# Moving a modulation's matrix-vector product from a dilated attention into the units of two feed-forwards

## The chip, the cores and the metric

The kernel runs on one core of a Trainium2 chip. The metric is the time of one execution on the device, in microseconds; the median of three runs of the kernel before is 3267.85 us (3267.14 to 3267.87).

## The reference

Two blocks work on x, 512 tokens of width 1024. The first has two layers, each of a feed-forward, a mixer and a second feed-forward, with a layer norm after each; the mixer is a pooling in layer 0 and a dilated attention in layer 1.

```python
for i in range(DEPTH):                          # DEPTH = 2
    h = _swiglu(x, ffn1_w_gate[i], ffn1_w_up[i], ffn1_w_down[i])
    x = _layer_norm(ALPHA * x + 0.5 * h, ...)
    m = _pool_mixer(...) if i % 2 == 0 else _dilated_attention_mixer(...)
    x = _layer_norm(ALPHA * x + m, ...)
    h = _swiglu(x, ffn2_w_gate[i], ffn2_w_up[i], ffn2_w_down[i])
    x = _layer_norm(ALPHA * x + 0.5 * h, ...)
```

The second block has two layers as well. Each begins with a modulation that depends on the vector c alone, not on x:

```python
mod = silu(c) @ ada_w[l] + ada_b[l]             # 1024 x 3072, l = 0, 1
shift, scale, gate = jnp.split(mod, 3, axis=-1)
h = rms_norm(x, pre_norm[l]) * (1.0 + scale) + shift
...
x = x + gate * rms_norm(y, post_norm[l])
```

So the modulation of both layers can be computed anywhere ahead of the second block. It is small: 24 MB of weights are read and multiplied once.

## The kernel before

**Stages.** The stages run one after the other; in the trace the first feed-forward lies at about 30 to 365 us, the pooling mixer up to 475, the second feed-forward of layer 0 up to 820, the first of layer 1 up to 1172, the dilated attention up to 1800, the last feed-forward up to 2160, then the second block. Tensors are fp32; every product is made as three matmuls of split operands (high and low parts), so TensorE has three matmuls for one product, and each weight must be split: ScalarE writes the high part (wh, L143), VectorE the low one (wl, L145), or GpSimd in one of five parts outside the units. `Stream` loads weights through the SP queue and keeps splits prepared four parts ahead of their use (`split_ahead`, five buffers).

**A feed-forward** (`ffn`, L476 to L601) has eleven units of 256 hidden columns, in four parts (`FF_PARTS`): units 0 to 2, 3 to 5, 6 to 8, 9 and 10. Unit 0 is a plain one (`first_unit`), in which VectorE also makes the sums of token blocks (`token_sums`). Units 1 to 10 use block sums: seven products (`product`, L512) of 24 matmuls of 256 columns each, for which VectorE makes four block sums (`block`, L108), seven splits and seven evacuations. After the units of a part, `f2` multiplies by w_down: two halves of 512 columns, TensorE's tiles t inside the rows kt. The last part's second half ends in the layer norm.

**The dilated attention** (`dilated_mixer`, L768) projects q, k and v for eight pairs of heads (`make_qk`, `make_v`) and attends beside it. For each pair `attend` goes through eight units of 128 queries: products (L880 to L886), scores on VectorE (L901, L904), the exponential on ScalarE (L905), a transposition on TensorE (L912), the weighing (L924, L928), the division (L933, L936) and a second transposition (L943).

**Background work.** `K.bg` takes a generator and a rate; `tick`, called after each three matmuls (as half a tick where they have 256 columns), advances it by the rate and runs the next step for each whole number. What a step issues stands there in the program. A planner then orders the instructions of each engine by when they can run by its own times; so an instruction without an early operand may float forward. `drain` runs what is left; generators with `slow` only when it is asked for these.

**The modulation** (`ada`, L1118 to L1170) is such a generator, started by `begin()` in the attention after the first projection, at 0.43 steps a tick, drained behind the attention. It goes through 24 blocks of 256 columns (12 for each layer). For a block it clears the sum m (L1141), reads the bias into its first row (L1142), and multiplies four quarters of two row tiles: a load of 256 KB through GpSimd's queue (L1132, two buffers adaw, each issued two quarters ahead) and two products on VectorE, whose first line is

```python
nc.vector.scalar_tensor_tensor(m, w[:, n, :], k.cols["c_2"][:, kt:kt + 1], m, ...)   # L1148
```

Then m is split (L1153, L1154), summed over the partitions by two matmuls with ones (L1161, L1162), a row is made on VectorE (L1165 to L1169) and stored (L1170). A block has seven yields; a layer has two more for the first loads. `pin` (L187) makes a tile depend on the latest output of a unit's `factor` in a feed-forward (`k.recent`) by a copy of one element on GpSimd; outside feed-forwards it does nothing.

Of the kernel before, what the change touches and what calls it, by code (L numbers as in the profile page):

```python
# [15 lines left out]
D = 1024  # L16
# [148 lines left out]
class K:  # L165
# [4 lines left out]
    def __init__(self, tc, ctx):  # L170
        self.tc = tc
        self.nc = tc.nc
        sp = lambda n, b, **k: ctx.enter_context(tc.tile_pool(name=n, bufs=b, **k))
        self.const = sp("const", 1)
        self.wraw = sp("wraw", self.raw_bufs)
        self.wraw2 = self.wsum = None
        self.wh = sp("wh", self.split_bufs)
        self.wl = sp("wl", self.split_bufs)
        self.ps = sp("ps", 8, space=PSUM)
        self.pend = []  # L180
        self.bgs = []
        self.recent = None

    def bank(self):
        return self.ps.tile([P, 512], F32, name="bank", tag="bank")
# [16 lines left out]

    def tick(self, w=1.0):
        for e in list(self.bgs):
            e[2] += e[1] * w
            while e[2] >= 1.0:
                e[2] -= 1.0
                try:
                    next(e[0])
                except StopIteration:  # L210
                    self.bgs.remove(e)
                    break
# [263 lines left out]
def ffn(k, st, a, name, i, lnj, post, tail=4):  # L476
    from contextlib import ExitStack
    nc, tc = k.nc, k.tc
    V = nc.vector
    with ExitStack() as ctx:  # L480
        sp = lambda n, b, c=ctx: c.enter_context(tc.tile_pool(name=n, bufs=b, reuse_waits="tile"))
        fa, ft = sp("ffa", 6), sp("fft", 2)
        units = ExitStack()
        k.wraw2, k.wsum, fs = sp("wraw2", k.raw_bufs, units), sp("wsum", 1, units), sp("ffs", 1, units)
        tmp = lambda n, dt: fa.tile([P, 2 * S], dt, name=n, tag="act")
        tp2 = lambda n, b=2: ft.tile([P, S], F32, name=n, tag=n, bufs=b)
        acts, A, later = {}, {}, []

        def new_acts(u):
            acts[u] = [tmp(n, F32R).rearrange("p (a b) -> p a b", a=2) for n in ("ah", "al")]  # L490

        def factor(u, v, o):

            h, lo = [o(x) for x in acts[u]]
            nc.scalar.activation(h, v, AF.Copy)
            V.tensor_tensor(lo, v, f32(h), ALU.subtract)
            k.recent = lo

        def first_unit():
            nonlocal A  # L500
            ps = f1_first(k, st, 4)
            A, later[:] = token_sums(k, fs, tmp)
            new_acts(0)
            for j in range(2):
                g = tp2("ta")
                nc.scalar.activation(g, ps[j], AF.Silu)
                ps[j] = g
            for j in range(2):
                V.scalar_tensor_tensor(ps[j], ps[j], 0.5, ps[2 + j], op0=ALU.mult, op1=ALU.mult)
                factor(0, ps[j], lambda x: x[:, j, :])  # L510

        def product(bank, name, first=False, last=False):  # L512

            h, lo = st.next()
            ah, al = A[name]
            for j in range(2):
                cs = slice(j * P, (j + 1) * P)
                o = bank[:, j * HS:(j + 1) * HS]
                for kt in range(4):
                    for n, (x, y) in enumerate(((h, ah), (h, al), (lo, ah))):  # L520
                        nc.tensor.matmul(o, x[:, kt, cs], y[:, kt, :], start=first and j == kt == n == 0,  # L521
                                         stop=last and kt == 3 and n == 2, skip_group_check=True)
                    k.tick(0.5)

        def unit(u, before):

            R, C = {}, {}
            b = k.bank()
            product(b, "a11", first=True)
            p1 = tp2("ta")  # L530
            nc.scalar.activation(p1, b, AF.Copy)
            before(0)
            ba = k.bank()
            product(ba, "a12", first=True, last=True)
            V.tensor_tensor(p1, p1, ba, ALU.add)
            nc.scalar.activation(p1, p1, AF.Silu)
            before(1)
            if later:
                later.pop(0)()
            product(b, "s2")  # L540
            u2 = tp2("tb")
            nc.scalar.activation(u2, b, AF.Copy)
            bc = k.bank()
            product(bc, "s1", first=True)
            product(b, "s3")
            u3 = tp2("tc")
            nc.scalar.activation(u3, b, AF.Copy)  # L547
            c22 = u3
            V.tensor_tensor(c22, u3, bc, ALU.add)
            if later:  # L550
                later.pop(0)()
            return b, bc, p1, u2, c22

        def rest(u, s, step):
            b, bc, g1, u2, c22 = s
            if u not in acts:
                new_acts(u)
            half = lambda n: lambda x: x[:, :, n * HS:(n + 1) * HS]
            two = lambda x: x.rearrange("p (a b) -> p a b", a=2)
            if step == 0:  # L560
                product(b, "a22", last=True)
                g2 = tp2("td", 1)
                nc.scalar.activation(g2, b, AF.Silu)
                V.scalar_tensor_tensor(c22, g2, 0.5, c22, op0=ALU.mult, op1=ALU.mult)
                factor(u, two(c22), half(1))
            else:
                product(bc, "s4", last=True)
                V.tensor_tensor(u2, u2, bc, ALU.add)
                V.scalar_tensor_tensor(u2, g1, 0.5, u2, op0=ALU.mult, op1=ALU.mult)
                factor(u, two(u2), half(0))  # L570

        for part, (u0, u1) in enumerate(FF_PARTS):
            fin = part == len(FF_PARTS) - 1
            if u0 == 0:
                first_unit()
            held = None
            for u in range(max(u0, 1), u1):
                s = unit(u, (lambda step: None) if held is None else (lambda step: rest(*held, step)))
                held = (u, s)
            rest(*held, 1)  # L580
            rest(*held, 0)
            if fin:
                units.close()
                k.wraw2 = k.wsum = None
                pl, tp = sp("ff", 1), sp("ffl", 2)
            for c in range(2):
                cs = slice(c * 512, (c + 1) * 512)
                if fin and c == 1:
                    G, B = load_gb(k, pl, a, i, lnj)

                def evac(t, ps):
                    x = k.x[t]
                    if part == 0:
                        V.scalar_tensor_tensor(x[:, cs], x[:, cs], ALPHA, ps, op0=ALU.mult, op1=ALU.add)
                    else:
                        V.tensor_tensor(x[:, cs], x[:, cs], ps, ALU.add)
                    if fin and c == 1:
                        k.pend.append(layer_norm_tile(k, tp, t, G, B, post))
                act = lambda kt: [x[:, kt % 2, :] for x in acts[kt // 2]]
                f2(k, st, act, list(range(2 * u0, 2 * u1)), 512, evac, tail=tail if fin and c == 1 else 0)  # L600
        k.recent = None  # L601

# [160 lines left out]
    return res  # L765


def dilated_mixer(k, st, a, lnj, begin):  # L768
    nc, tc = k.nc, k.tc
    slopes = alibi_slopes()  # L770
    with tc.tile_pool(name="dmo", bufs=1, reuse_waits="tile") as po:
        oT = [po.tile([P, S], F32, name=f"oT{i}") for i in range(KT)]
        with tc.tile_pool(name="dm", bufs=1, reuse_waits="tile") as pl, \
# [183 lines left out]
            for kind, n in DIL_ORDER:  # L957
# [3 lines left out]
                    make_qk(n)  # L961
                made.add((kind, n))
                k.drain()
                if len(made) == 1:
                    begin()
                hp = 2 * n if kind == "v" else n
                if ("v", hp // 2) in made and ("qk", hp) in made:
                    last = len(made) == len(DIL_ORDER)
# [149 lines left out]
def ada(k, a, l, out, alloc):  # L1118
# [16 lines left out]
    yield  # L1135
    load(1)
    yield
    for j in range(3 * D // W):
        i, c = j * W // D, j * W % D
        m = alloc("adam", F32)  # L1140
        nc.gpsimd.memset(m, 0.0)  # L1141
        nc.gpsimd.dma_start(m[0:1, :], a["ada_b_2"][l:l + 1, j * W:(j + 1) * W])  # L1142
        for q in range(4):
            yield
            w = loads.pop(4 * j + q)
            for n in range(2):
                kt = 2 * q + n
                nc.vector.scalar_tensor_tensor(m, w[:, n, :], k.cols["c_2"][:, kt:kt + 1], m,  # L1148
                                               op0=ALU.mult, op1=ALU.add)
            load(4 * j + q + 2)  # L1150
        yield
        h, lo = alloc("adah", F32R), alloc("adal", F32R)
        nc.scalar.activation(h, m, AF.Copy)  # L1153
# [701 lines left out]
def program(tc, a, out):  # L1855
    from contextlib import ExitStack
    with ExitStack() as ctx:
# [66 lines left out]
        for i in range(DEPTH):  # L1924
# [2 lines left out]
            ffn(k, st, a, "ffn1", i, 0, to_xT(k, dilated))  # L1927
            if dilated:
                k.drain()
                dilated_mixer(k, st, a, 1, lambda: k.bg(modulation(), 0.43, slow=True))  # L1930
                k.drain(slow=True)
            else:
                pool_mixer(k, st, a, 1)
            if last:
                begin_mod()
            ffn(k, st, a, "ffn2", i, 2, to_b2 if last else to_xT(k))
        k.drain()
        R = Rest()
# [92 lines left out]
```

## Time and profile before

| | |
|---|---|
| median of the runs | 3267.85 us (3267.14 to 3267.87) |
| profiled execution, its own time | 3268.62 us |
| its span in the trace | 3266.6 us |
| granted clock, mean | 0.995 |
| busy: TensorE, VectorE, ScalarE, GpSimd | 98%, 67%, 42%, 13% |

A busy share is an average over stages. Matmuls are pipelined and their ends modelled, so what counts for TensorE is where it is idle, what ended the idle time, and what clock was granted. Idle time of another engine costs only where TensorE waits behind it.

### The profile page before, as it was taken

Reading aid. Unit: us, or ns where it says so; the run is one execution under the profiler, and the core shown is the slowest. Engines: PE = TensorE matmul, PEld = TensorE weight load, DVE = VectorE, ACT = ScalarE, POOL = GpSimd, SP = SyncE. Lnnn points to the kernel's source line nnn. Section 1 sums busy time; section 2 is a strip of 40 time slices with the busy share of each in tenths; the row PEclk is TensorE's granted clock in tenths of the full one; section 3 lists DMA queues with packets and bytes.
Section 4 is the critical chain, followed back from the end, with each engine's and each line's share of the span. In section 5 each row is a group of like instructions: output and inputs, shape, how many; then the busy total and the mean of one; then the engine's idle time right before and its main releaser. Section 6 shows DMA issues by size and latency. Waiting matters only on the chain.

```text
span 3266.6 us, 51461 instructions
## 1 busy us (share of the span) xinstructions
PE 3203.7 (98%) x21325; PEld 2753.0 (84%) x21325; DVE 2178.3 (67%) x3517; ACT 1359.8 (42%) x2025; POOL 439.0 (13%) x528
## 2 busy tenths in 40 slices
PE   8999999999999999999999999989999999999999
PEld 8999889998999987778777999977778788777877
DVE  8866877767877555565655966666965646695563
ACT  5444334443444334444443544433434533343442
POOL 1000110000000022333421100021121001112000
PEclk9999999999999999999999999999999999999999
DMA  5332332332332333433432422332122322121222
GB/s 171 123 102 91 104 117 91 117 117 78 119 101 87 101 97 98 123 115 106 127 105 74 144 94 93 104 101 97 59 78 91 104 97 100 66 98 65 80 89 78
DMA packets 279953, 326.65 MB, mean 100 GB/s; under 512 B 11860, under 2 KB 224056, under 8 KB 279720
## 3 DMA queue, kind: packets, MB, share of 16 engines
q1 hardware_dynamic: 268632, 294.36, 27.5%
q0 software_dynamic: 10944, 28.95, 2.9%
q8 instruction: 167, 2.74, 0.3%
q14 instruction: 66, 0.54, 0.1%
q10 hardware_dynamic: 144, 0.07, 0.0%
HBM read 317.02 MB, written 6.32 MB: 99 GB/s over the span
## 4 chain that ended last, share of the span: by engine, by line
PE 72%; DVE 9%; issue 3%; DMA 2%; POOL 1%; ACT 1%; DVEq 0%; POOLq 0%; ACTq 0%
PE bank L521 18%; PE bank L225 16%; PE bank L227 15%; PE bank L226 15%; DVE wl L145 1%; DVE work L1337 1%; DVE m L1336 1%; DMA adaw<-in_ada_w_dram 1%; PE bank L912 1%; PE bank L1299 1%; PE bank L1644 1%; PE bank L886 1%; PE bank L1626 1%; DVE adam L1148 1%; PE bank L924 1%
## 5 line engine op out<-in xcount | busy, mean ns | idle before, releaser
L143 ACT ACTIVATE wh<-wraw 128x1024 fp32r<-128x1024 f32 (+1 forms) x608 | 637.6, 1052 | 929.3 <-PE bank L227 284.5
L145 DVE TENSOR_TENSOR wl<-wraw,wh 128x1024 fp32r<-128x1024 f32 (+1 forms) x535 | 662.3, 1240 | 513.0 <-ACT wh L143 501.2
L225 PE MATMUL bank<-xTh,wh 128*128 128x512 f32 (+1 forms) x1344 | 504.3, 376 | 2.9 <-ACT wh L143 1.7
L226 PE MATMUL bank<-xTl,wh 128*128 128x512 f32 (+1 forms) x1344 | 490.9, 366 | 2.8 <-DVE ve L354 1.5
L227 PE MATMUL bank<-xTh,wl 128*128 128x512 f32 (+1 forms) x1344 | 491.2, 366 | 1.5 <-DVE wl L145 1.5
L145 POOL TENSOR_TENSOR wl<-wraw,wh 128x1024 fp32r<-128x1024 f32 (+1 forms) x73 | 179.7, 2462 | 1965.3 <-ACT wh L143 1703.9
L225 PE MATMUL bank<-wh,xTh 128*128 128x512 f32 (+2 forms) x1024 | 371.7, 363 | 1.5 <-ACT xTh L346 1.5
L226 PE MATMUL bank<-wl,xTh 128*128 128x512 f32 (+2 forms) x1024 | 363.5, 355 | 2.0 <-DVE wl L145 2.0
L227 PE MATMUL bank<-wh,xTl 128*128 128x512 f32 (+2 forms) x1024 | 364.4, 357 | 0.0
L521 PE MATMUL bank<-xTh,wh 128*128 128x256 f32 x1280 | 360.0, 281 | 0.1
L521 PE MATMUL bank<-xTl,wh 128*128 128x256 f32 x1280 | 358.4, 280 | 0.0
L521 PE MATMUL bank<-xTh,wl 128*128 128x256 f32 x1280 | 358.4, 280 | 0.0
L225 PEld LDWEIGHTS bank<-xTh,wh 128*128 128x128 f32 x1344 | 254.9, 190 | 59.4 <-issue 15.8
L227 PEld LDWEIGHTS bank<-xTh,wl 128*128 128x128 f32 x1344 | 255.4, 190 | 46.2 <-DVE wl L145 1.7
L226 PEld LDWEIGHTS bank<-xTl,wh 128*128 128x128 f32 x1344 | 256.4, 191 | 40.4 <-DVE ve L354 2.1
L225 PE MATMUL bank<-wh,ah 128*128 128x512 f32 x704 | 275.1, 391 | 1.2 <-ACT wh L143 1.0
L227 PE MATMUL bank<-wh,al 128*128 128x512 f32 x704 | 274.7, 390 | 0.0
L226 PE MATMUL bank<-wl,ah 128*128 128x512 f32 x704 | 274.4, 390 | 0.2 <-POOL wl L145 0.2
L521 PEld LDWEIGHTS bank<-xTh,wh 128*128 128x128 f32 x1280 | 241.0, 188 | 5.6 <-ACT tc L547 5.1
L521 PEld LDWEIGHTS bank<-xTl,wh 128*128 128x128 f32 x1280 | 241.0, 188 | 0.6
L521 PEld LDWEIGHTS bank<-xTh,wl 128*128 128x128 f32 x1280 | 240.9, 188 | 0.0
L225 PEld LDWEIGHTS bank<-wh,xTh 128*128 128x128 f32 x1024 | 192.9, 188 | 32.0 <-ACT xTh L346 2.4
(410 smaller groups left out, 5971.9 us busy)
## 6 DMA issues: line engine op xcount, KB each, us to landing
wraw<-in_w_in_dram SPq DMA_DIRECT2D x58, 1024.0 KB, 4.8
wraw<-in_ffn_w_up_dram SPq DMA_DIRECT2D x43, 1024.0 KB, 5.0
wraw<-in_ffn_w_gate_dram SPq DMA_DIRECT2D x43, 1024.0 KB, 5.0
wraw<-in_ffn_w_down_dram SPq DMA_DIRECT2D x32, 1024.0 KB, 4.9
wraw<-in_attn_w_qkv_dram SPq DMA_DIRECT2D x56, 512.0 KB, 3.7
adaw<-in_ada_w_dram POOLq DMA_DIRECT2D x96, 256.0 KB, 3.3
wraw<-in_ffn_w_down_dram SPq DMA_DIRECT2D x24, 512.0 KB, 4.1
wraw<-in_attn_w_qkv_dram SPq DMA_DIRECT2D x8, 1024.0 KB, 5.0
```

The costliest lines, as they stand in the source:

```text
L143: nc.scalar.activation(h, raw, AF.Copy)
L145: (nc.gpsimd if pool else nc.vector).tensor_tensor(lo, raw, f32(h), ALU.subtract)
L225: nc.tensor.matmul(ps, s[0], m[0], start=start, stop=False)
L226: nc.tensor.matmul(ps, s[0], m[1], start=False, stop=False)
L227: nc.tensor.matmul(ps, s[1], m[0], start=False, stop=stop)
L521: nc.tensor.matmul(o, x[:, kt, cs], y[:, kt, :], start=first and j == kt == n == 0, stop=last and kt == 3 and n == 2, skip_group_check=True)
L886: nc.tensor.matmul(ps[g - 1][r * 32:(r + 1) * 32, 256:], q[g][:, r * P + i * 32:r * P + (i + 1) * 32], kk[g][:, :, r * P:(r + 1) * P], sta ...
L912: nc.tensor.transpose(ps[:, j * P:(j + 1) * P], p[:, j * P:(j + 1) * P], k.ident)
L924: nc.tensor.matmul(ps[c:c + 64, :E], t[:, j * P + c:j * P + c + 64], v0[:, i + j, hh, :], start=j == 0, stop=False, tile_position=(0, c))
L1148: nc.vector.scalar_tensor_tensor(m, w[:, n, :], k.cols["c_2"][:, kt:kt + 1], m, op0=ALU.mult, op1=ALU.add)
L1299: k.nc.tensor.matmul(ps[:, :n], q, ks[i][:, g, :n], start=i == 0, stop=i == 1)
L1336: nc.vector.max(out=m8, in_=cur[:, :n])
```

## The change

The modulation leaves the dilated attention. It is now started ahead of the second feed-forward of layer 0, at half the rate (0.215), and drained ahead of the dilated attention, so that it runs in two feed-forwards. A flag `hold` stops slow background work in a feed-forward's first unit and in the multiplication by w_down of its last part. In `ada`, a block's sum is cleared and its bias read (`begin(j + 1)`) after the second quarter of the block before. The first product of each quarter is tied by `keep_in_program_order` behind the instruction that was traced before it on VectorE: an order, no wait; it can't float forward any more. The second product follows the first through m. As `k.recent` is set in a feed-forward, each load now has the copy of `pin` ahead of it.

```diff
--- before.py
+++ after.py
@@ -180,6 +180,7 @@
         self.pend = []
         self.bgs = []
         self.recent = None
+        self.hold = False
 
     def bank(self):
         return self.ps.tile([P, 512], F32, name="bank", tag="bank")
@@ -202,6 +203,8 @@
 
     def tick(self, w=1.0):
         for e in list(self.bgs):
+            if e[3] and self.hold:
+                continue
             e[2] += e[1] * w
             while e[2] >= 1.0:
                 e[2] -= 1.0
@@ -571,8 +574,10 @@
 
         for part, (u0, u1) in enumerate(FF_PARTS):
             fin = part == len(FF_PARTS) - 1
+            k.hold = u0 == 0
             if u0 == 0:
                 first_unit()
+                k.hold = False
             held = None
             for u in range(max(u0, 1), u1):
                 s = unit(u, (lambda step: None) if held is None else (lambda step: rest(*held, step)))
@@ -583,6 +588,7 @@
                 units.close()
                 k.wraw2 = k.wsum = None
                 pl, tp = sp("ff", 1), sp("ffl", 2)
+            k.hold = fin
             for c in range(2):
                 cs = slice(c * 512, (c + 1) * 512)
                 if fin and c == 1:
@@ -599,6 +605,7 @@
                 act = lambda kt: [x[:, kt % 2, :] for x in acts[kt // 2]]
                 f2(k, st, act, list(range(2 * u0, 2 * u1)), 512, evac, tail=tail if fin and c == 1 else 0)
         k.recent = None
+        k.hold = False
 
 
 
@@ -765,7 +772,7 @@
     return res
 
 
-def dilated_mixer(k, st, a, lnj, begin):
+def dilated_mixer(k, st, a, lnj):
     nc, tc = k.nc, k.tc
     slopes = alibi_slopes()
     with tc.tile_pool(name="dmo", bufs=1, reuse_waits="tile") as po:
@@ -961,8 +968,6 @@
                     make_qk(n)
                 made.add((kind, n))
                 k.drain()
-                if len(made) == 1:
-                    begin()
                 hp = 2 * n if kind == "v" else n
                 if ("v", hp // 2) in made and ("qk", hp) in made:
                     last = len(made) == len(DIL_ORDER)
@@ -1135,19 +1140,30 @@
     yield
     load(1)
     yield
+    def begin(j):
+
+        if j < 3 * D // W:
+            sums[j] = alloc("adam", F32)
+            nc.gpsimd.memset(sums[j], 0.0)
+            nc.gpsimd.dma_start(sums[j][0:1, :], a["ada_b_2"][l:l + 1, j * W:(j + 1) * W])
+
+    sums = {}
+    begin(0)
     for j in range(3 * D // W):
         i, c = j * W // D, j * W % D
-        m = alloc("adam", F32)
-        nc.gpsimd.memset(m, 0.0)
-        nc.gpsimd.dma_start(m[0:1, :], a["ada_b_2"][l:l + 1, j * W:(j + 1) * W])
+        m = sums.pop(j)
         for q in range(4):
             yield
             w = loads.pop(4 * j + q)
             for n in range(2):
                 kt = 2 * q + n
-                nc.vector.scalar_tensor_tensor(m, w[:, n, :], k.cols["c_2"][:, kt:kt + 1], m,
-                                               op0=ALU.mult, op1=ALU.add)
+                ins = nc.vector.scalar_tensor_tensor(m, w[:, n, :], k.cols["c_2"][:, kt:kt + 1], m,
+                                                     op0=ALU.mult, op1=ALU.add)
+                if n == 0:
+                    k.tc.keep_in_program_order(ins)
             load(4 * j + q + 2)
+            if q == 1:
+                begin(j + 1)
         yield
         h, lo = alloc("adah", F32R), alloc("adal", F32R)
         nc.scalar.activation(h, m, AF.Copy)
@@ -1927,12 +1943,14 @@
             ffn(k, st, a, "ffn1", i, 0, to_xT(k, dilated))
             if dilated:
                 k.drain()
-                dilated_mixer(k, st, a, 1, lambda: k.bg(modulation(), 0.43, slow=True))
                 k.drain(slow=True)
+                dilated_mixer(k, st, a, 1)
             else:
                 pool_mixer(k, st, a, 1)
             if last:
                 begin_mod()
+            else:
+                k.bg(modulation(), 0.215, slow=True)
             ffn(k, st, a, "ffn2", i, 2, to_b2 if last else to_xT(k))
         k.drain()
         R = Rest()
```

## Rows read from the trace of the kernel before

**Rows 1.** The page, head: span, and busy time of TensorE and VectorE.

```profile
span 3266.6 us, 51461 instructions
...
PE 3203.7 (98%) x21325; PEld 2753.0 (84%) x21325; DVE 2178.3 (67%) x3517; ACT 1359.8 (42%) x2025; POOL 439.0 (13%) x528
```

**Rows 2.** Windows of two stages: length, busy us (count), clock, DMA share, GB/s.

```profile
475.00:820.00 345.00, 343.77 (x2405) 320.34 (x2403) 252.84 (x273) 146.99 (x180) 16.81 (x8) 1.00 0.32 104
...
1172.00:1800.00 628.00, 613.04 (x4956) 489.46 (x4955) 356.73 (x765) 267.24 (x411) 187.97 (x294) 0.99 0.35 105
```

**Rows 3.** Windows by cycle of the dilated attention, from transposition L865 to the next.

```profile
1212.10:1293.90 81.80, 81.80 (x681) 67.22 (x680) 38.29 (x81) 36.48 (x56) 18.30 (x28) 1.00 0.31 90
1293.90:1355.90 62.00, 59.05 (x489) 44.11 (x487) 42.23 (x93) 27.77 (x45) 25.85 (x42) 1.00 0.39 116
...
1437.80:1503.00 65.20, 60.68 (x491) 45.59 (x490) 40.14 (x94) 28.22 (x44) 23.19 (x39) 0.97 0.41 123
...
1584.80:1647.60 62.80, 60.12 (x488) 45.12 (x487) 41.14 (x95) 28.06 (x43) 27.06 (x43) 0.97 0.38 118
1647.60:1737.80 90.20, 85.39 (x683) 69.77 (x682) 48.89 (x103) 39.30 (x63) 21.05 (x29) 0.96 0.39 124
```

**Rows 4.** Waits of TensorE in the dilated stage: us in total, times, longest.

```profile
PE bank L912 <- ACT sc L905: 11.2, 6, 2.7
PE bank L943 <- DVE on L936: 2.3, 2, 2.1
```

**Rows 5.** Windows at half clock in the dilated stage, three of four.

```profile
1463.40:1466.80 3.40, 3.40 (x10) 2.62 (x9) 3.11 (x7) 1.94 (x3) 1.40 (x3) 0.50 0.00 0
...
1596.50:1599.90 3.40, 2.75 (x9) 2.36 (x10) 3.34 (x6) 3.35 (x6) 1.25 (x2) 0.50 0.25 76
...
1726.20:1729.60 3.40, 3.40 (x11) 2.82 (x10) 1.53 (x4) 0.60 (x1) 0.11 (x1) 0.51 0.42 131
```

**Rows 6.** Waits of VectorE in the dilated stage, the two of the modulation.

```profile
DVE adam L1148 <- DMA adaw<-in_ada_w_dram: 49.6, 31, 4.3
DVE adam L1148 <- DMA adam<-in_ada_b_dram: 43.5, 16, 5.4
```

**Rows 7.** Timeline of VectorE around one stall: start, us, what, idle before it.

```profile
1594.14 0.48 DVE L1148 SCALAR_TENSOR_TENSOR adam<-adaw,cols,adam 128x256 f32<-128x256 f32 x1 [3.70 <-DMA adaw<-in_ada_w_dram]
1594.54 1.14 DVE L901 SCALAR_TENSOR_TENSOR sc<-dist,bank 128x256 f32<-128x256 f32 x4
```

**Rows 8.** Tile adam in the dilated stage: ns min/median/max, first and last start.

```profile
L1148 DVE SCALAR_TENSOR_TENSOR adam<-adaw,cols,adam x176: 467/485/2510, 1267.3 to 1729.8; 128x256 f32<-128x256 f32 x176
...
L1154 DVE TENSOR_TENSOR adal<-adam,adah x23: 394/426/3112, 1261.7 to 1737.7; 128x256 fp32r<-128x256 f32 x23
...
L1165 DVE COPY adam<-bank x8: 402/406/414, 1259.5 to 1580.0; 1x256 f32<-1x256 f32 x8
```

**Rows 9.** Tile adaw there: its loads, issue to landing.

```profile
DMA to landing us min/median/max: 3.0/3.3/5.5
```

**Rows 10.** Windows of units: first part of two feed-forwards, second part of one.

```profile
40.40:80.00 39.60, 38.57 (x322) 38.24 (x321) 39.53 (x59) 22.38 (x30) 2.80 (x4) 1.00 0.34 107
495.60:535.00 39.40, 39.40 (x330) 39.04 (x329) 35.92 (x38) 21.70 (x28) 2.41 (x1) 1.00 0.37 121
568.20:631.00 62.80, 62.80 (x518) 61.97 (x517) 47.84 (x49) 32.63 (x41) 2.41 (x1) 1.00 0.35 118
```

**Rows 11.** Waits of TensorE in the first part of the first feed-forward.

```profile
PE bank L225 <- ACT wh L143: 1.0, 1, 1.0
```

**Rows 12.** Tile adaw in that stretch, products of the modulation floated there.

```profile
L1148 DVE SCALAR_TENSOR_TENSOR adam<-adaw,cols,adam x16: 474/485/2506, 57.9 to 101.0; 128x256 f32<-128x256 f32 x16
```

**Rows 13.** One window of the start.

```profile
8.00:10.00 2.00, 0.83 (x4) 0.43 (x3) 1.68 (x3) 1.73 (x3) 0.00 (x0) 1.00 1.09 413
```

**Rows 14.** GpSimd by line in the two feed-forwards, its smallest operation.

```profile
L782 POOL MEMSET v<- 128x4 f32 x8 | 0.3, 102 | 0.0
```

**Rows 15.** GpSimd by line in the dilated stage, one with a copy.

```profile
L822 POOL CAST k<-k 64x512 fp32r<-64x512 f32 x14 | 8.7, 620 | 44.5 <-ACT k L819 44.1
```

## Prediction

> **What bounds the kernel now.** I read the page first: TensorE is busy 3203.7 of 3266.6 us, VectorE 67% [rows 1]. So a change can win only where TensorE stands idle or runs slowly, at most some 63 us of idle time, and it loses wherever it makes TensorE wait. Then the windows of the two stages that the change touches [rows 2]: the feed-forward that receives the modulation has TensorE busy 343.77 of 345 us, the dilated stage 613.04 of 628. All the modulation's gain must come from those last 15 us and what hangs on them.
>
> Third, I cut the dilated stage at the five transpositions of L865, one cycle for each pair of heads [rows 3]. There are two kinds, with the projection of v and without. The three long ones take 81.8, 81.9 and 81.8 us with TensorE busy throughout; the first of them stands in the rows. They all run beside the modulation, or part of it, and lose nothing. The three short ones take 62.0, 65.2 and 62.8 us with 2.95, 4.52 and 2.68 us idle; the last, a long one, takes 90.2 with 4.81 idle. The idle sum is 14.96 us. Of it 11.2 us are six waits of the transposition L912 for the exponential and 2.3 are waits for the head's output [rows 4]; the rest is one wait of 1.4 us for another copy.
>
> Why are those late? VectorE takes its instructions in order. In this stage it stands 49.6 us before L1148 for the weights of the modulation and 43.5 us for its bias row [rows 6]. One place shows the chain: VectorE idles 3.70 us until adaw has landed, does its product at 1594.14, and only then the scores at 1594.54 [rows 7], which the exponential and TensorE's 2.68 us wait are behind. That is the link between the modulation and TensorE's idle time: the long wait stands ahead of the scores in one queue.
>
> Idle time has a second price here. Four windows of 3.4 us, each just after such a stall, have a granted clock of 0.5, which is the level of 1.2 GHz; three are filled with matmuls, one has 2.75 us of them [rows 5]. Half of 3.4 + 2.75 + 3.4 + 3.4 is 6.5 us lost. The cycles agree: 62.0 - 2.95, 65.2 - 4.52 - 1.7 and 62.8 - 2.68 - 1.4 give 59.05, 58.98 and 58.7, and 90.2 - 4.81 - 3.4 gives 82.0 against 81.8.
>
> **The change part by part.** *Removed from the dilated stage:* 176 products L1148 and their waits. TensorE gets back 14.96 + 6.5 = **21.5 us**. The modulation's own matmuls (two of 256 columns for each of 24 column blocks) only move, from one stage in which TensorE is full to another: nothing. What is late next there is TensorE itself, as in the long cycles. At half the effect this is 10.8 us; I take the whole, since three cycles of 82 us already run without a loss.
>
> *Removed from the start:* today 16 of the 192 products float to 57.9 to 101.0 us [rows 12], and with them two 256 KB loads at the very start. VectorE is full in that stretch (39.53 of 39.60 us) and TensorE waits 1.0 us once, while the same part of the next feed-forward has no wait [rows 10, 11]. With the first product tied to its place that is gone: **1.0 us**. The two loads stood among others that moved 413 GB/s [rows 13]; 0.52 MB at this rate are 1.3 us by which first weights might come earlier. Between 0 and 1.3 I take **1.0**, for TensorE was waiting for just these.
>
> *Moved earlier: the bias row.* begin(j + 1) after the second quarter puts memset and transfer some five steps ahead of their use. The 43.5 us [rows 6] vanish wherever the work lies.
>
> *Added to the feed-forwards.* A block takes 7 steps of the generator, 24 blocks and four extra steps make 172. A feed-forward has 10 units outside the hold x 7 products x 4 = 280 ticks, and 3 x 48 = 144 in the parts' second halves, 424 in all; at 0.215 that is 91 steps, 182 in both. It suffices, and the drain ahead of the attention has nothing left. VectorE's price of a block is 8 x 0.485 + 0.426 + 0.406 = 4.71 us [rows 8]; 24 of them are 113 us. A tick is six matmuls of 256 columns: 39.4 us with 330 matmuls [rows 10] give 0.119 each, 0.72 a tick. In a window of units, 62.8 us with VectorE busy 47.84 [rows 10], there are 88 ticks, 18.9 steps, 2.7 blocks: 12.7 us. That makes 60.5 of 62.8 us: it fits, with 2.3 us to spare, and the second halves of the parts are freer still. The work hides beside TensorE. In the first part VectorE has 35.92 of 39.4 us [rows 10], and 12 steps, 8 us of it at most, go in: there it is over full, as it is today in the first feed-forward, where 16 products and an idle of VectorE for their loads cost TensorE 1.0 us [rows 11, 12]. Two such parts: 2 us by the nearest row. Nothing at the low end, as splits are prepared four parts ahead; at the high end I let each lose 5 us, about the work that does not fit (35.92 + 8 - 39.4). I take 2 and add 1 for TensorE waiting for the modulation's split sum in a part where VectorE is behind: **3 us, between 0 and 10**.
>
> *The new wait and who stands behind it.* Each product still waits for its load, and the units' splits, block sums and evacuations wait behind it. A load is issued when the product two steps before has freed its buffer: two steps are 9.3 ticks, 6.7 us, against 3.3 us to landing, at most 5.5 [rows 9]. In the attention the rate was 0.43, half this distance, which is why it missed. GpSimd gets one small copy more for each of 96 loads (pin), ahead of the transfer; the nearest operations are 0.10 us for a tiny memset and 0.62 for a copy of 64x512 [rows 14, 15]. I take 0.10, for it is one element. On GpSimd's queue its splits of weights stand behind such a copy and behind the load's wait for a freed buffer; they have the four parts of preparation to spare.
>
> A rule speaks against these copies. In the first feed-forward one product of VectorE took 2506 ns instead of 485, beside a split of weights on GpSimd [rows 12]. The Trainium skill (SBUF — State Buffer, section on who shares ports with whom) states that a VectorE instruction with two SBUF inputs and a GpSimd instruction that reads SBUF exclude each other for the whole instruction. The 2506 ns agree. By it each of 96 copies could hold VectorE; this is the fourth rival below.
>
> **Sum.** Against the profiled span of 3266.6: -21.5 - 1.0 - 1.0 + 3.0 = 3246.1. The median of the runs, 3267.85, lies 1.25 above the span (the profiled execution itself took 3268.62), so 3247.3.
>
> **The rivals.** *First, slower: VectorE runs dry in the units.* The loads miss their products in the feed-forward as well. The tight ones are the third and fourth quarter of each block, 48; two thirds of the ticks lie in units, so 32. Eight windows of units have 2.3 us to spare each, 18 in all. A mean wait w costs 32w - 18. At 1.6 us, the mean of the 31 waits of today [rows 6], this is 33 us, on 3244.3: **3277**. It decides from w = 1.3 us. For it: VectorE is nearly full. Against: twice the distance, and landings of 3.3.
>
> *Second: half of the stalls stay.* The attention's chain of scores, exponential and transposition may be late by its splits as well. Then 10.8 us are not won: **3258**. Against it stand the long cycles without idle.
>
> *Third: the change does not do what it says.* Only the first product of a pair is tied, and only against floating forward; the rest may slip into the held places, two first units and two last parts. A pair is 0.97 us and a landing 3.3 [rows 8, 9]; four places are 17 us: **3264**.
>
> *Fourth: the copies on GpSimd hold VectorE.* At 0.62 us [rows 15], 96 are 60 us, 39 of it in units, less 18 to spare: 21 us on 3244.3, **3265**. At 0.10 it is 6 us and hidden.
>
> **How the numbers follow.** Forecast 0.66, first rival 0.12, second 0.10, third 0.07, fourth 0.05. This kernel's runs tell a difference of about 0.2%, 6.5 us: faster is below 3261.3 (forecast and second, 0.76), slower above 3274.4 (first, 0.12), the rest 0.12. The forecast's bounds are 3244 (no cost, the whole start) and 3254 (feed-forwards lose 10); short cycles that agree within 0.35 us, eight times, take the low end to 3241. To hold 8 in 10 the upper end goes past the second rival: 3241 to 3262.
>
> **What would show it.** Right: the dilated stage 20 us shorter, short cycles near 59 us, the last near 82, no window at half clock there; no L1148 before 500 us; VectorE's waits for adam gone and those for adaw well under 49.6 us; the two feed-forwards longer by 3 us at most together. Wrong: waits of TensorE for wl or wh in the units, VectorE waiting for adaw there by over 1.3 us a time, or TensorE still idle before L912.

## The result and the profile after

| | before | after |
|---|---|---|
| median of the runs | 3267.49 us | 3292.26 us (3288.88 to 3294.72) |
| ratio | | 1.0078 (interval 1.0065 to 1.009) |
| profiled execution: its time, its span | 3268.62, 3266.6 us | 3291.62, 3289.8 us |

The kernel became 25 us slower. The forecast was 3247 and the range ended at 3262; of the rivals only the first, "VectorE runs dry in the units" (3277), had forecast a slower kernel. The median of before is now that of four runs. The line numbers moved: L1148 is now L1160 (product), L1132 is L1137 (load), L521 is L524 (matmul of a unit), and the copy of `pin` is L192.

For the stages I cut both traces at the last row block of each layer norm (us; in brackets the idle time of TensorE and the length of its windows at half clock):

| stage | before | after | difference |
|---|---|---|---|
| first feed-forward, layer 0 | 373.0 | 372.9 | -0.1 |
| pooling | 104.9 | 105.9 | +1.0 |
| second feed-forward, layer 0 | 352.0 (1.8; 0) | 379.1 (18.4; 10.2) | +27.1 |
| first feed-forward, layer 1 | 348.3 (3.0; 0) | 370.0 (16.0; 6.8) | +21.7 |
| dilated attention | 633.4 (16.5; 13.7) | 605.5 (1.6; 3.4) | -27.9 |
| last feed-forward | 358.1 | 359.6 | +1.5 |
| second block | 1097.0 | 1096.9 | -0.1 |

The attention gave back what was expected; the two feed-forwards, forecast at +3, took 48.8. Of these, 29.6 us are idle time of TensorE (34.4 - 4.8). In the 17.0 us at half clock TensorE was busy for 15.7, and half of that is 7.9. The 24 pairs of matmuls of the modulation, at some 0.235 us a pair, are 5.6, which only moved. The last 6 us I can't place.

Windows of after, columns as in [rows 2]: length, busy us of TensorE, its loads, VectorE, ScalarE, GpSimd, granted clock, DMA share, GB/s. They cover most of the two feed-forwards and the attention, then the stretches of [rows 10] from 495.6 and 568.2.

```profile
475.00:845.00 370.00, 353.30 (x2426) 327.66 (x2424) 299.42 (x394) 148.21 (x190) 140.82 (x156) 0.99 0.41 134
845.00:1224.00 379.00, 361.36 (x2497) 335.38 (x2497) 311.14 (x409) 152.91 (x197) 102.19 (x146) 0.99 0.40 128
1224.00:1820.00 596.00, 596.00 (x4879) 475.06 (x4879) 248.99 (x535) 259.28 (x387) 83.94 (x122) 1.00 0.24 72
...
495.60:535.00 39.40, 38.25 (x321) 37.93 (x320) 39.40 (x48) 22.35 (x28) 17.52 (x14) 1.00 0.41 125
...
568.20:631.00 62.80, 58.12 (x454) 56.65 (x452) 52.86 (x71) 28.29 (x37) 23.13 (x28) 0.97 0.38 124
```

The attention has no idle time left (596.00 of 596, against 613.04 of 628 in [rows 2]). In the units TensorE has lost 4.68 of 62.80 us, and VectorE, which should be the late one, is busy for 52.86 of them only. It isn't overloaded; it stands. The waits in the two feed-forwards say where (engine, tile, line <- what came last: total us, times, longest); first VectorE, then ScalarE, then TensorE:

```profile
DVE adam L1160 <- DMA adaw<-in_ada_w_dram: 73.1, 30, 6.0
...
ACT adah L1169 <- DVE adam L1160: 94.2, 18, 9.4
...
PE bank L524 <- ACT tb L545: 8.7, 8, 2.0
PE bank L524 <- DVE tc L552: 6.2, 3, 3.6
PE bank L1177 <- ACT adah L1169: 4.8, 3, 2.0
PE bank L524 <- ACT tc L550: 3.6, 3, 1.8
```

The wait of [rows 6] for the weights of the modulation was 49.6 us in 31 times; it moved with the products and grew to 73.1 in 30, 2.4 us each. The wait for the bias row, 43.5 us, is gone. How the first becomes idle time of TensorE is seen at 812.6 us, at the first load of the modulation's second layer. VectorE, then TensorE (start us, us, what, idle before it and what ended it), then the window at half clock that begins in TensorE's stall:

```profile
813.67 1.00 DVE L1160 SCALAR_TENSOR_TENSOR adam<-adaw,cols,adam 128x256 f32<-128x256 f32 x2 [5.91 <-DMA adaw<-in_ada_w_dram]
814.59 1.22 DVE L145 TENSOR_TENSOR wl<-wraw,wh 128x1024 fp32r<-128x1024 f32 x1
815.72 0.68 DVE L552 TENSOR_TENSOR tc<-tc,bank 128x512 f32<-128x512 f32 x1
```

```profile
812.59 0.28 PE L524 MATMUL bank<-xTh,wl 128*128 128x256 f32 x1
816.46 0.58 PE L524 MATMUL bank<-s4h,wh 128*128 128x256 f32 x1 [3.59 <-DVE tc L552]
...
815.10:818.50 3.40, 2.04 (x9) 2.05 (x10) 2.18 (x4) 0.00 (x0) 1.48 (x2) 0.50 0.23 65
```

VectorE waits 5.91 us for a load that only the modulation needs. Behind the product in its queue stand a split and L552, which reads a bank of a unit before TensorE may add the next product to that bank. TensorE stands 3.59 us, and works at half clock (0.50). By the program a unit lets this read be late by about one product (24 matmuls at 0.119 us, 2.8 us).

Of the 30 waits, eight have a stall of TensorE within 6 us behind them, 13.4 us together. The others do not stop TensorE at once, but a wait can leave VectorE late for longer. After the longest one, which ends at 595.29, VectorE has no pause over 0.1 us up to 609.21, and TensorE stands twice. VectorE, TensorE, then ScalarE:

```profile
595.29 1.00 DVE L1160 SCALAR_TENSOR_TENSOR adam<-adaw,cols,adam 128x256 f32<-128x256 f32 x2 [6.01 <-DMA adaw<-in_ada_w_dram]
...
598.08 0.39 PE L524 MATMUL bank<-s4h,wh 128*128 128x256 f32 x1 [2.26 <-DVE tc L552]
...
609.21 0.39 PE L524 MATMUL bank<-xTh,wh 128*128 128x256 f32 x1 [1.99 <-ACT tb L545]
...
608.05 0.63 ACT L498 ACTIVATE ah<-tb 128x512 fp32r<-128x512 f32 x1 [1.54 <-DVE tb L572]
608.58 0.58 ACT L545 ACTIVATE tb<-bank 128x512 f32<-128x512 f32 x1
```

The second stall comes through ScalarE, which waits for VectorE's L572 and has the copy L545 of another bank behind that. The 8.7 us above are eight such stalls, four behind L572 and four behind VectorE's L538. Not all is the loads' doing: around 909 to 916 us, in the first part of the next feed-forward, TensorE stands 3.9 us, and no product has waited for its load for over 90 us.

### The profile page after: what moved, and what is told of

Its sections match the earlier page's. It is cut to its first block, busy times and chain, and to the rows that moved or that the text cites. A ratio compares the mean times of both kernels' runs of the same rounds, so it can differ in the third digit from the quotient of the medians.

```text
span 3289.8 us, 51573 instructions
## 1 busy us (share of the span) xinstructions
PE 3214.0 (98%) x21325; PEld 2760.2 (84%) x21325; DVE 2162.4 (66%) x3517; ACT 1357.2 (41%) x2025; POOL 532.2 (16%) x624
## 4 chain that ended last, share of the span: by engine, by line
PE 56%; DVE 6%; issue 2%; DMA 1%; POOL 1%; ACT 1%; DVEq 0%; POOLq 0%; ACTq 0%
PE bank L228 14%; PE bank L230 13%; PE bank L229 13%; PE bank L524 7%; DVE wl L145 1%; PE bank L919 1%; DVE work L1353 1%; PE bank L893 1%; DVE m L1352 1%; PE bank L931 1%; PE bank L1315 1%; PE bank L935 1%; PE bank L1660 1%; PE bank L1642 1%; DMA wraw<-in_w_in_dram 0%
## 5 line engine op out<-in xcount | busy, mean ns | idle before, releaser
L524 PE MATMUL bank<-xTh,wh 128*128 128x256 f32 x1280 | 361.8, 283 | 12.7 <-ACT tb L545 8.7
L524 PE MATMUL bank<-xTh,wl 128*128 128x256 f32 x1280 | 359.4, 281 | 0.2 <-DVE wl L145 0.2
L524 PE MATMUL bank<-xTl,wh 128*128 128x256 f32 x1280 | 359.3, 281 | 0.0
L228 PEld LDWEIGHTS bank<-xTh,wh 128*128 128x128 f32 x1344 | 255.1, 190 | 60.0 <-issue 15.8
L524 PEld LDWEIGHTS bank<-xTh,wh 128*128 128x128 f32 x1280 | 242.0, 189 | 19.6 <-ACT tb L545 10.3
L524 PEld LDWEIGHTS bank<-xTl,wh 128*128 128x128 f32 x1280 | 241.8, 189 | 0.6
L524 PEld LDWEIGHTS bank<-xTh,wl 128*128 128x128 f32 x1280 | 241.9, 189 | 0.4 <-DVE wl L145 0.4
```

Of the source, the lines that this page charges most:

```text
L228: nc.tensor.matmul(ps, s[0], m[0], start=start, stop=False)
```

## Experiments

The theory, A in the texts of expectations: the loads come too late, VectorE stands before the products, and what is behind it in its queue comes late to TensorE. Its rivals: B, the modulation's work does not fit beside VectorE's own in the feed-forwards; C, the new copies on GpSimd hold VectorE itself up. Below, "loss" is the length of the two feed-forwards less the 700.3 us of before, 48.8 in after, and "waits" are those of VectorE for adaw in them; both are read from one profiled execution, while the measured time is a median of 4 to 11 runs. Ratios are to runs of before made beside them (medians 3267.22 to 3268.75). Edits are made to the kernel after, but for one.

**e1. The loads four quarters ahead instead of two**

```diff
-            load(4 * j + q + 2)
+            load(4 * j + q + 4)     # and four buffers adaw, four first loads
```

> The changed kernel with four buffers adaw instead of two: each load is issued four quarters ahead of its products, all of VectorE's work stays. Theory A (VectorE stands in order before a product whose load has not landed): its waits for adaw in the two feed-forwards fall from 73.1 us to under 15, and of the 43 us that these lost some 25 to 35 come back: 3258 to 3268 us. Theory B (the 113 us of VectorE work itself do not fit beside the units): the waits fall, the time does not: 3285 to 3294 us. Theory C (the copies on GpSimd ahead of each load hold VectorE): as B.

Measured: 3262.38 us, ratio to before 0.998 (0.997 to 0.9989); loss 19.1 us. The wait of 73.1 us in 30 times has shrunk to this:

```profile
DVE adam L1162 <- DMA adaw<-in_ada_w_dram: 0.7, 1, 0.7
```

All products, splits and copies are still there, and 30 us are back. That is A. The longest stall left, 3.77 us at 989 before the same L552, stands behind a wait of VectorE for a row of pre_norm:

```profile
990.78 0.41 DVE L1185 SCALAR_TENSOR_TENSOR adam<-bank,adam 1x256 f32<-1x256 f32 x1 [5.79 <-DMA adam<-in_pre_norm_dram]
```

**e2. One load for all products of a layer**

```diff
-        if j < 3 * D // W:
+        if n == 0:                  # and w = loads[0] for every product
```

> Of each layer's 48 loads of weights only the first is made, with its copy on GpSimd; every product reads that tile, so most of the weights are left out of the sum. All VectorE work stays, in its place; no load can be late, and 94 of 96 copies and transfers are gone. Theory A: 3250 to 3260 us. Theory B: 3280 to 3294 us. Theory C: as A. Against the kernel with four buffers this tells what copies and transfers still cost once no load is late.

Measured: 3257.31 us, ratio 0.9965 (0.9952 to 0.9978), loss 12.5, waits 0.3. With the work on VectorE whole, but no loads and copies, the change is a gain: A again, and against B.

**e3. Products of 8 columns instead of 256**

```diff
-                ins = nc.vector.scalar_tensor_tensor(m, w[:, n, :], k.cols["c_2"][:, kt:kt + 1], m,
+                ins = nc.vector.scalar_tensor_tensor(m[:, :8], w[:, n, :8], k.cols["c_2"][:, kt:kt + 1], m[:, :8],
```

> The products of the modulation work on 8 columns instead of 256, so most of the sum is left out; loads, copies and the order stay. VectorE's work falls by some 80 us, the waits for loads stay possible. Theory A: the waits for adaw stay at 50 us or more and with them most of the loss: 3275 to 3290 us. Theory B: 3244 to 3255 us.

Measured: 3289.01 us, ratio 1.0061 (1.0046 to 1.0076), loss 47.6. A product (ns min/median/max) and the wait:

```profile
L1160 DVE SCALAR_TENSOR_TENSOR adam<-adaw,cols,adam x192: 204/222/2328, 509.9 to 1146.9; 128x8 f32<-128x8 f32 x192
...
DVE adam L1160 <- DMA adaw<-in_ada_w_dram: 59.8, 28, 4.8
```

A product takes 222 ns in place of 478, and nothing is won: while the loads are late, VectorE's work is not the limit. B falls as the main cause.

**e4. No copies on GpSimd**

```diff
             w = alloc("adaw", F32)
-            k.pin(w)
```

> The changed kernel without the copy on GpSimd ahead of each load. A load follows its freed buffer directly, about 1.3 us sooner (0.98 us of copy, 0.3 to the issue). Theory A: the waits for adaw fall by a third to a half, 3270 to 3285 us. Theory B: 3285 to 3294 us. Theory C: 3250 to 3265 us, and VectorE's operations of two inputs lose their long outliers.

Measured: 3261.49 us, ratio 0.9977 (0.9968 to 0.9986), loss 18.0. By the time alone this is C's number, and A's price for the copies was too low. The rows decide between them, first two of after, then those of this kernel:

```profile
L1160 DVE SCALAR_TENSOR_TENSOR adam<-adaw,cols,adam x192: 462/478/2592, 510.9 to 1152.4; 128x256 f32<-128x256 f32 x192
...
L145 DVE TENSOR_TENSOR wl<-wraw,wh 128x1024 fp32r<-128x1024 f32 x164 | 201.3, 1229 | 20.0 <-ACT wh L143 20.0
...
L1159 DVE SCALAR_TENSOR_TENSOR adam<-adaw,cols,adam x192: 462/480/3194, 509.3 to 1118.6; 128x256 f32<-128x256 f32 x192
...
L145 DVE TENSOR_TENSOR wl<-wraw,wh 128x1024 fp32r<-128x1024 f32 x168 | 206.6, 1231 | 42.8 <-ACT wh L143 42.7
...
DVE adam L1159 <- DMA adaw<-in_ada_w_dram: 28.7, 18, 3.5
```

If the copies held VectorE, its operations would be shorter without them. The longest product is 3194 ns (2592 in after), and splits have a mean of 1231 ns (1229 in after). What went is 61% of the wait for the loads, 73.1 to 28.7. So C falls as a mechanism, and the copies do cost most of the loss: ahead of a load in GpSimd's queue, they make it late. They do so in two ways, which this run does not part. In after, 12 waits (32.4 us) stand behind copies that took over 1 us. Eight more (20.5 us) stand behind copies that had first waited for the unit's output al (L499), to which `pin` ties the load.

**e9. Four ahead, and copies for the first four loads only**

> The changed kernel with four buffers and a copy ahead of the first four loads alone: the kernel with all parts together without its wider hold and without the high part on VectorE. If late loads are the loss and the first part's full VectorE costs little, it is within 4 us of that kernel: 3249 to 3255 us. If the first part matters (idle of 4 us and two windows at half clock were left there in the second feed-forward with four buffers): 3255 to 3262 us.

Measured: 3253.49 us, ratio 0.9954 (0.9939 to 0.9969), loss 13.9, waits 0.0: the first range. With the runs above, this prices the wait. The profiled execution took 3258.23 us, the other three 3253.08 to 3253.72, so I give its differences twice, by losses and by medians. Without copies, 28.7 us of waits of VectorE cost 18.0 - 13.9 = 4.1 us, or 8.0 by the medians; with copies, 72.4 us more of them cost 48.8 - 19.1 = 29.7, or 29.9. A microsecond of waits that last 3.5 us at most costs less than one of waits that reach 6.0. Copies that no product waits for still cost 19.1 - 13.9 = 5.2, or 8.9: the stall of 3.77 us at 989 is gone here. In e1 the row that it waited for was issued at 985.66 us, on GpSimd's queue, behind a copy that took 2.57 us.

What stays lies in the first parts. Windows of this kernel, the first part in either feed-forward:

```profile
495.60:535.00 39.40, 38.26 (x320) 37.92 (x319) 39.40 (x48) 22.72 (x29) 10.35 (x14) 1.00 0.44 139
865.00:905.00 40.00, 35.90 (x259) 34.17 (x259) 36.70 (x46) 19.46 (x26) 9.04 (x11) 0.96 0.52 165
```

TensorE is idle for 1.14 and 4.10 us. In the second, from 882.4 to 894.0 us, VectorE goes from one operation to the next without a gap, and one of its products takes 2.59 us beside a split of weights on GpSimd (next lines, VectorE and GpSimd); TensorE's second stall, 1.88 us, stands behind the sum that this product ends.

```profile
890.51 2.59 DVE L1163 SCALAR_TENSOR_TENSOR adam<-adaw,cols,adam 128x256 f32<-128x256 f32 x1
...
889.41 3.41 POOL L145 TENSOR_TENSOR wl<-wraw,wh 128x1024 fp32r<-128x1024 f32 x1 [1.60 <-ACT wh L143]
```

**e5. The high part of the sum on VectorE instead of ScalarE**

```diff
-        nc.scalar.activation(h, m, AF.Copy)
+        nc.vector.tensor_copy(h, m)
```

> The changed kernel with the high part of a block's sum (adah) made on VectorE instead of ScalarE, where it waited 94 us for the products. The question is by which way VectorE's waits for loads reach TensorE. Theory S (through ScalarE: adah stands in its queue, the copies of the units' partial sums behind it, and TensorE's next product into the same bank waits for these): the loss shrinks by half or more, 3262 to 3275 us, TensorE's waits for tb and tc on ScalarE fall from 12 to under 5 us. Theory D (directly: VectorE's own evacuations and splits are late): 3284 to 3294 us.

Measured: 3291.24 us, ratio 1.0075 (1.0061 to 1.0088), loss 51.9, waits 74.4. ScalarE stood 94.2 us behind the modulation's sum in after, yet to take that away gives nothing, and the waits for tb stay. The stall reaches TensorE through VectorE's own queue, directly and by what ScalarE needs from it for the units:

```profile
PE bank L524 <- ACT tb L545: 8.8, 8, 2.3
PE bank L524 <- DVE tc L552: 8.3, 6, 2.8
```

**e6. Before, with the bias row read early** (`begin(j + 1)` after the second quarter, as in after; nothing else)

> The kernel before with one part of the change alone: a block's sum is cleared and its bias read after the second quarter of the block before; the modulation stays in the attention, untied. My account of the kernel before gives its 43.5 us of VectorE's waits for the bias about half of the 21.5 us that the modulation costs TensorE there: 3255 to 3261 us, waits for adam under 5 us. If the waits for adaw take their place (the load of the next quarter then ends the same wait): 3264 to 3270 us.

Measured: 3268.31 us, ratio 1.0004 (0.9995 to 1.0012). The waits of VectorE in the attention, and one of GpSimd:

```profile
DVE adam L1155 <- DMA adaw<-in_ada_w_dram: 46.9, 32, 4.2
DVE adam L1155 <- DMA adam<-in_ada_b_dram: 46.3, 17, 6.5
...
POOL adam L1142 <- DMA md<-adam: 29.0, 15, 6.3
```

The time lies in the second range, but not for its reason: the waits for the bias are all there. The row is asked for earlier in the program and arrives no earlier: 2.07 us after its issue VectorE starts the product, and the issue still comes 7.2 us after the last product of the block before (medians; 2.04 and 6.9 in before). With two buffers adam the memset has to wait until the sum before has been stored. In after the bias is issued 12.0 us ahead of that last product and lands 9.8 ahead (medians). There a block has twice the ticks; that this is why is argued, not tested.

**e7. No tie to VectorE's program order** (the two lines of `keep_in_program_order` removed)

> The changed kernel without the tie of each quarter's first product to its place. If the tie is part of the cause (it sets a product ahead of ready work of the units), VectorE's waits for adaw fall under 50 us and the time to 3265 to 3285 us. If the tie only keeps products from floating forward, they can float no further than their loads allow, which their copies hold to the place: 3285 to 3296 us, with waits as before or longer.

Measured: 3346.86 us, ratio 1.0244 (1.0228 to 1.026), loss 109.9, waits:

```profile
DVE adam L1160 <- DMA adaw<-in_ada_w_dram: 114.7, 53, 6.8
```

Worse than either expectation. The tie is worth 55 us here; without it VectorE waits more often and longer for the loads. It is the part of the change that works.

**e10. A wider hold alone** (no modulation in any unit of the first part; rate 0.25 for 0.215)

> The changed kernel with two buffers and all its copies, and the wider hold alone (no modulation in the first part's units, rate 0.25). If the loss is the full VectorE of the first part, it falls by half: 3262 to 3275 us. If late loads are the loss, the higher rate brings the loads closer to their products and the waits for adaw grow over 73 us: 3288 to 3305 us.

Measured: 3298.37 us, ratio 1.009 (1.0072 to 1.0108), loss 55.3, waits 80.4. To run the same work denser in the freer parts makes the waits for loads longer and gains nothing.

**e8. All together:** four ahead, copies for the first four loads, high part on VectorE, the wider hold at 0.25

> The changed kernel with four buffers, a copy ahead of the first four loads alone, the high part on VectorE, and the hold extended over the first part's units (rate 0.25 instead of 0.215, so that it still ends in time). If the loads' waits, ScalarE's wait and the first part's full VectorE are all there is to the loss, the feed-forwards lose little more than the 5.6 us of the modulation's own matmuls that moved there: 3244 to 3254 us. If VectorE's work itself costs something in the other parts: 3256 to 3264 us.

Measured: 3249.57 us, ratio 0.9951 (0.9938 to 0.9963): faster than both kernels. Loss 8.5, of which 5.6 are the matmuls that moved. The wait, and two windows of after in this kernel:

```profile
DVE adam L1163 <- DMA adaw<-in_ada_w_dram: 5.3, 3, 2.7
...
495.60:535.00 39.40, 39.40 (x330) 39.05 (x329) 36.05 (x38) 22.41 (x28) 2.40 (x1) 1.00 0.36 116
568.20:631.00 62.80, 62.73 (x517) 61.79 (x516) 57.06 (x79) 31.04 (x39) 15.86 (x21) 1.00 0.51 164
```

VectorE is now busy for 57.06 us of the stretch of units, more than in after, and TensorE for 62.73 of 62.80. So the work does hide in the units, as soon as nothing in the queue waits. With the first part left free, TensorE has 39.40 of its 39.40 us there. Whether this step gains over e9 is not shown: the medians are 3.9 us apart, but the intervals of the ratios, 0.9938 to 0.9963 and 0.9939 to 0.9969, cover each other. Its three further edits were not parted; e5 alone and e10 alone gained nothing. Four buffers in the attention, the place of before, would have asked the other question; this was not tried.

## Why the prediction was wrong

**The dilated stage: right.** Forecast -21.5; measured -27.9, less the 5.6 us of matmuls that moved away, -22.3. Idle time went from 16.5 to 1.6 us, half clock from 13.7 to 3.4. To read the loss from the short cycles against the long ones [rows 3 to 5] was sound.

**The matmuls: nothing, as said.** They left one full stage for another, 5.6 us each way.

**The start: -2.0 forecast, nothing measured.** The stage is 372.9 long for 373.0. The 16 floated products are gone (first L1160 at 510.9 us), and with them two loads; TensorE was idle 0.9 us less there (10.2 for 11.2), but the stage did not get shorter; why is open.

**The feed-forwards: the step that failed.** "3 us, between 0 and 10" was 43 net of the matmuls. Its two parts fared differently. The work of VectorE in the units hides, as summed (e8). For the two first parts, with the wait for the modulation's own sum, 3 us were taken, and e9, with no late load, has 1.1 + 4.1 = 5.2: a size. What failed is "The new wait": two steps of 6.7 us against 3.3 to landing, and both sides of it were wrong. The way was taken as the transfer alone. From the end of the product that frees the buffer to the landing of the load, in the two feed-forwards of after (means, us):

| quarter that the load is for | copy starts after product | copy | to issue | issue to landing | waits |
|---|---|---|---|---|---|
| third | 0.26 | 1.66 | 0.30 | 3.75 | 15, 44.5 us |
| fourth | 2.48 | 0.64 | 0.30 | 4.03 | 12, 19.3 us |

These sum to 6.0 and 7.5 us; over half of the 2.48 comes from five copies that waited for al (L499). And the distance was shorter than 6.7: in e2, where no load can be late, VectorE comes to a third quarter 4.1 us after the product two quarters ahead of it and to a fourth after 4.7 (medians, the same in e1 and e9; 1.1 at the least), to the other two, with the steps of the block's end between, after 14.4 and 15.8. An even pace of the steps was taken, and VectorE's order does not keep it; why is not shown. With 3.0 us to landing at the least, some loads miss such a turn without any copy, the 28.7 us of e4. The first two quarters had three waits in all; 27 of the 30 lie in the two quarters that the rival named as the tight ones. The copy was taken at 0.10 us "for it is one element", between 0.10 and 0.62; its mean is 0.98.

A second premise was missing. "The work hides beside TensorE" weighed busy time against length. TensorE adds several products into one bank with VectorE's and ScalarE's reads between them, so it waits when a single one of these is late by more than about 2.8 us, however idle the engine is in the mean. Eight of the 30 waits lead to that within 6 us; the longest leaves VectorE behind, so that a second read is late 14 us after it.

**The first rival: right in kind.** It decides from a mean wait of 1.3 us, and the mean was 2.4. By its formula the 30 waits give 73.1 - 18 = 55 us on 3244.3, 3299; 3292.26 was measured. The slack of 18 us was too small: of the 72.4 us of waits between e1 and after, 42.7 cost nothing. Its chance of 0.12 was held down by the comparison above.

**The other rivals.** Half of the stalls did not stay: TensorE has no wait from 1224 to 1820 us, in the attention. Nothing slipped into the held places: no L1160 starts between 816.8 and 880 us, in the last part's w_down and the next first unit. The fourth had the right object and the wrong loser: not VectorE but the copy is held, and it costs more than the 21 us given, through the loads (after against e4, 30.8 us).

**The bias row.** Its wait vanished, but "wherever the work lies" is wrong: in the attention the same edit leaves 46.3 us of it (e6).

## What to carry to other kernels

Background work with loads of its own is safe in an in-order engine's queue only if each load lands before its consumer's turn; count the whole way from the freed buffer to the landing, with everything ahead of the load on the issuing queue, and hold it against the shortest distance between the consumer's turns in the trace, not the mean. Where TensorE accumulates into a bank that another engine reads in between, ask how long that engine may stand still once, not only how busy it is. An operation of one element on GpSimd ahead of a load is not free beside a VectorE that works without a pause.

## What was not expected of the hardware

The copy of one element (`pin`), issued 96 times in after, takes 0.173 us at the least; 47 of them took over 0.5 us, 84.4 us together, and every one of the 47 ended within 0.08 us of the end of an operation of VectorE. The tile's row (ns min/median/max), then GpSimd and VectorE at one place:

```profile
L192 POOL COPY adaw<-al x96: 173/427/4914, 500.2 to 1147.7; 1x1 f32<-1x1 f32 x96
...
596.37 1.10 POOL L192 COPY adaw<-al 1x1 f32<-1x1 f32 x1 [4.77 <-DVE adam L1160]
...
596.21 1.22 DVE L145 TENSOR_TENSOR wl<-wraw,wh 128x1024 fp32r<-128x1024 f32 x1
```

The copy starts inside VectorE's split and ends 0.04 us after it (597.47 against 597.43); the split has its usual 1.22 us. The Trainium skill (SBUF — State Buffer, "SBUF: two separate sides") says that of two such instructions (one of VectorE with two inputs in SBUF, one of GpSimd that reads SBUF) the one that starts first has the shared ports for its whole instruction and the other blocks. The trace agrees. The prediction drew on the same rule and saw VectorE as the one that is held. But beside all of the 47 an operation of VectorE was running when the copy started, and the loser is the small instruction. It can lose several times in a row. Six copies ahead of a third quarter's load took 4.0 to 4.2 us, and each stood through five operations of VectorE. Here is one, with VectorE beside it:

```profile
560.06 4.18 POOL L192 COPY adaw<-al 1x1 f32<-1x1 f32 x1 [0.24 <-DVE adam L1160]
...
559.93 1.21 DVE L145 TENSOR_TENSOR wl<-wraw,wh 128x1024 fp32r<-128x1024 f32 x1
561.06 0.47 DVE L1160 SCALAR_TENSOR_TENSOR adam<-adaw,cols,adam 128x256 f32<-128x256 f32 x1
561.46 1.21 DVE L122 TENSOR_TENSOR wraw<-wraw 128x1024 f32<-128x1024 f32 x1
562.59 0.47 DVE L1160 SCALAR_TENSOR_TENSOR adam<-adaw,cols,adam 128x256 f32<-128x256 f32 x1
562.99 1.21 DVE L124 TENSOR_TENSOR wraw<-wraw 128x1024 f32<-128x1024 f32 x1
```

Each operation of VectorE starts 0.07 to 0.08 us before the one ahead of it has ended, and the copy ends 0.04 us after the last of the five. It goes the other way where GpSimd's instruction is the long one: the product of 2.59 us in e9 has the split of 3.41 us beside it.
